# Where the ordinary weight steps stand inside a group of matrix products, how many of them run ahead, and how many tiles of the next group may be loaded

## The chip, the cores and the metric

The kernel runs on one core of one Trainium2 chip. TensorE multiplies, VectorE (DVE) and ScalarE (ACT) work element by element, GpSimd (POOL) and SyncE (SP) mostly issue transfers. The metric is the device time of one execution in microseconds; lower is better. The kernel before took 2078.74 us, the median of three runs between 2076.82 and 2080.69.

## The reference

One layer, 256 rows (tokens) of 2048 numbers, all in float32. A first SwiGLU feed-forward, then attention and retention in parallel with their gates, then a second feed-forward, and a final norm:

```python
def swiglu_ffn(x, w_gate, w_up, w_down):
    return (jax.nn.silu(x @ w_gate) * (x @ w_up)) @ w_down

x = x + 0.5 * swiglu_ffn(rmsnorm(x, norm_ffn1_g), w1_gate, w1_up, w1_down)
h = rmsnorm(x, norm_mix_g)
proj = h @ w_in            # q, k, v of both mixers, and three gates
...
x = x + merged @ w_out
x = x + 0.5 * swiglu_ffn(rmsnorm(x, norm_ffn2_g), w2_gate, w2_up, w2_down)
return rmsnorm(x, norm_final_g)
```

The feed-forwards have 5632 hidden columns. All the weights are read once, some 490 MB.

## The kernel before, in words

**A step.** Every product of activations and weights is cut into steps that hold one weight tile of 256 rows by 512 columns, in SBUF as 128 partitions x 1024 numbers (512 KB). A step's weights are split in two parts: `hi` by a cast on ACT (L128) and `lo`, the rest, by a subtraction on DVE (L129). TensorE then makes three products, `hi` with both parts of the activations (L139, L140) and `lo` with the first (L142). A *standard step* (function `standard`) does this for both halves of 128 rows, twelve matmuls; its tile arrives by a transfer on SP's queue into one of five raw buffers (`RAW_BUFS`).

**A group.** For 10 of the 11 column blocks of each feed-forward, and for the gates of the mixing part, the kernel uses Strassen's scheme on a pair of products (class `Strassen`): seven half-size products in place of eight, at the price of sums of weight tiles. A group has four phases. Phases 0, 1 and 2 have eight *group steps* each, of two kinds that alternate (r: of an operand as it is, s: of a sum), phase 3 has four of kind s. A group step has six matmuls. Its first operands are eight tiles in SBUF, four `k` and four `x`, loaded on POOL's queue (L542). Two of the `x` tiles get the other operand added by an accumulating transfer (L546), the other two by DVE (`first`, L531). In phase 1 each pair also costs DVE an addition (L593) and a subtraction (L579), and POOL an accumulating transfer (`third`, L580). At the end of phase 0 ACT copies PSUM bank `c` away (L636) before phase 1 goes on adding to that bank. After phases 1, 2 and 3 the results are scaled, put through SiLU and multiplied (L639, L642, L650, L653, L765, L768), and a few steps into the next group they are transposed and split as activations (`Operand.put`, L378, L379, L384). These are the operands of the down product.

**The weave.** `weave` writes the order out. It puts `lead` standard steps first, then the groups, and after each pair of group steps it adds to a credit and, if that is high enough, lays in one standard step. So a group has 16 places: four pairs in each of phases 0 to 2 and four single steps in phase 3. The weights of the places are the tuple `SHARE`; the place at the end of phase 2 (`turn`) always gets a step if there is one. In a feed-forward the standard steps are those of the one plain block (gate, then up: 8 steps each), then the down products: 11 passes, one for each column block, of 4 jobs with 2 steps each. A pass may only start some steps after its block's results are there (`at_hand`). A job's second step ends it: ACT then moves two banks out and puts two new ones in, four operations (L785, L788). Fourteen standard steps stay behind the last group. The mixing part has its own lead and shares.

**Running ahead.** `run` goes through the steps in order. Before the matmuls of step c it emits the splits of up to four steps ahead (four `hi`/`lo` buffers, `SPLIT_BUFS`), and with them what else the step's `prep` holds. All engines work their instructions off in this order. `load_some` issues transfers as far as there is room: five raw tiles, and for the groups' first operands as many tiles as `room["kept"]` says. A tile's room comes back when its last split has been emitted, in phases 2 and 3. The tiles themselves come from a pool of 30 (`ACT_TILES`), shared with the 16 parts of the normed activations and with the operands of the down products. The first group's loads may not start before step `first`.

Of the kernel before, what the change touches and what calls it, by code (L numbers as in the profile page):

```python
# [18 lines left out]
D = 2048  # L19
# [7 lines left out]
NB = 512  # L27
KC = 2
# [3 lines left out]
RAW_BUFS = 5  # L32
SPLIT_BUFS = 4
KEPT = 8
ACT_TILES = 30
TAIL = 4
AHEAD = (2, 3)
HALF_K = D // P // 2
LEAD = 12
MIX_LEAD = 8  # L40
RET_WAIT = (14, 5)
HELD = 6

MIX_SHARE = (0.85,) * 4 + (1.0,) * 4 + (0.8,) + (0.4,) * 3 + (0.15,) * 4
SHARE = (0.7,) * 2 + (0.2,) * 2 + (1.3,) * 4 + (0.3,) * 4 + (0.2,) * 4
ADDED = (2, 3)
PLAIN = 10
PASSES = ((10,),) + tuple((b,) for b in range(10))
# [26 lines left out]
def block_kernel(ctx: ExitStack, tc: tile.TileContext, x, g1, w1g, w1u, w1d, gm, w_in, rel, woa, wor, wo,  # L75
# [5 lines left out]
    wpool = ctx.enter_context(tc.tile_pool(name="weights", bufs=1))  # L81
    apool = ctx.enter_context(tc.tile_pool(name="acts", bufs=ACT_TILES))
    tmp = ctx.enter_context(tc.tile_pool(name="tmp", bufs=4))
# [13 lines left out]
    def tmp_tile(name, tag="t", bufs=None):  # L97
        return tmp.tile([P, NB], F32, tag=tag, name=name, bufs=bufs)


    steps = []
    transfers = []
    kept = []
    state = {"dma": 0, "kept": 0, "prep": 0, "step": 0, "slots": SPLIT_BUFS}
    room = {"raw": RAW_BUFS, "kept": KEPT}
    due = {}

    def later(n, fn):
        due.setdefault(state["step"] + n, []).append(fn)
# [114 lines left out]
    def load_some():  # L224
        while state["dma"] < len(transfers) and room["raw"]:
            room["raw"] -= 1
            transfers[state["dma"]]()
            state["dma"] += 1
        while state["kept"] < len(kept) and room["kept"] and kept[state["kept"]][0] <= state["step"]:
            room["kept"] -= 1  # L230
            kept[state["kept"]][1]()
            state["kept"] += 1
# [427 lines left out]
    def down_done(b, factor, after):  # L660
        def done(acc):
            for t in range(NT):
                xb = xs[t][:, b * NB : (b + 1) * NB]
                nc.vector.scalar_tensor_tensor(xb, acc[t], factor, xb, op0=ALU.mult, op1=ALU.add)
            if after is not None:
                after(b)

        return done
# [8 lines left out]

        return done

    def weave(jobs, apart, groups, lead, share, start=None):  # L680


        queue = [(job, k) for job in jobs for k in range(0, job.nk, KC)]
        at_hand = {}

        def next_standard():

            if len(queue) <= apart:
                return False
            job, k = queue[0]  # L690
            if any(at_hand.get(b, len(steps) + 1) > len(steps) for b in job.needs):
                return False
            steps.append(standard(job, k))
            del queue[0]
            if job.makes is not None and k + KC == job.nk:
                at_hand[job.makes] = len(steps) + 6
            return True

        for _ in range(lead):
            next_standard()  # L700
        rate = (len(queue) - apart) / (len(groups) * sum(share))
        credit = 0.0
        first = len(steps) - 8
        for n, (b, make) in enumerate(groups.items()):
            group = make()
            loads = group.loads()
            if start is not None and n == 0:
                loads[0] = lambda load=loads[0]: [start(), load()]
            kept.extend((first + i if n == 0 else 0, fn) for i, fn in enumerate(loads))
            for i, part in enumerate(group.steps()):  # L710
                steps.extend(part)
                credit += rate * share[i]
                if i + 1 == len(share):
                    at_hand[b] = len(steps) + 7

                turn = i + 1 == 3 * (HALF_K // KC)
                if (turn or credit >= (0.2 if (i + 1) % (HALF_K // KC) == 0 else 0.6)) and next_standard():
                    credit -= 1
        for job, k in queue:
            steps.append(standard(job, k))  # L720

    def ffn(name, norm, wg, wu, wd, after, start=None):


        nblocks = DFF // NB
        mids, ready = {}, {}

        def put_mid(b, hs):
            mids[b] = Operand(f"{name}a{b}", 1)
            for t in range(NT):  # L730
                mids[b].put(0, t, hs[t])

        def plain(b):
            gates = {}

            wait = GATE_WAIT if start is not None and b == PLAIN else 0

            def gate_done(acc):
                def go():
                    for t in range(NT):  # L740
                        gates[t] = tmp_tile(f"{name}g{b}{t}", "gate", 2)
                        nc.scalar.activation(gates[t], acc[t], AF.Silu, scale=norm.scale(t))

                if wait:
                    later(wait, go)
                else:
                    go()

            def up_done(acc):
                for t in range(NT):  # L750
                    a = gates[t]
                    nc.vector.scalar_tensor_tensor(a, acc[t], norm.scale(t), a, op0=ALU.mult, op1=ALU.mult)  # L752
                later(4, lambda: put_mid(b, gates))

            tags = ("acc", "acc")
            up = Gemm(wu, 0, b * NB, D // P, norm, up_done, tags)
            up.makes = b
            return [Gemm(wg, 0, b * NB, D // P, norm, gate_done, ("z", "z") if wait else tags), up]

        def paired(b):  # L760
            got = {}

            def evict(t, side, r):
                if side == 1:
                    nc.scalar.activation(r, r, AF.Silu)  # L765
                    got[t] = r
                    return
                nc.vector.scalar_tensor_tensor(got[t], r, norm.scale(t), got[t], op0=ALU.mult, op1=ALU.mult)  # L768
                if t == 1:
                    later(4, lambda: put_mid(b, got))  # L770

            return Strassen(norm, wu, b * NB, wg, b * NB, evict, ADDED)

        def down(blocks, last):

            jobs = []

            def act(k, t):
                return mids[blocks[k // 4]](k % 4, t)

            for b in range(D // NB):
                cols = slice(b * NB, (b + 1) * NB)

                def seed(acc, t, cols=cols):
                    nc.scalar.activation(acc, xs[t][:, cols], AF.Copy, scale=2.0)  # L785

                def evict(acc, t, cols=cols):
                    nc.scalar.activation(xs[t][:, cols], acc, AF.Copy, scale=0.5)  # L788

                if last:  # L790
                    job = Gemm(wd, 0, b * NB, 4 * len(blocks), act, down_done(b, 0.5, after))
                else:
                    job = Gemm(wd, 0, b * NB, 4 * len(blocks), act, None, ("acc", "acc"), seed)
                    job.evict = evict
                job.rows = [(m * 4 + i) * P for m in blocks for i in range(4)]
                job.needs = blocks
                jobs.append(job)
            return jobs

        downs = {blocks: down(blocks, blocks is PASSES[-1]) for blocks in PASSES}  # L800
        jobs = plain(PLAIN) + [job for p in PASSES for job in downs[p]]
        for job, follow in zip(jobs, jobs[1:]):
            job.next = follow
        groups = {b: (lambda b=b: paired(b)) for b in range(nblocks) if b != PLAIN}
        weave(jobs, len(downs[PASSES[-1]]) * len(PASSES[-1]) * 4 // KC + HELD, groups, LEAD, SHARE, start)


    n1 = Norm("n1", gains[:, 0, :], True)
# [3 lines left out]
    def third_block():  # L812

        there = small.tile([P, NB // P], F32, tag="there", name="there", bufs=1)
        nc.gpsimd.tensor_tensor(there, n1.raw[2][:, 0, : NB // P], mhalf, op=ALU.mult)

    ffn("f1", n1, w1g[0], w1u[0], w1d[0], x_updated(nm), third_block)


# [210 lines left out]
    def gates(col1, col2, func, dsts):  # L1030


        def evict(t, side, r):
            if side == 1:
                nc.scalar.activation(r, r, func)
            else:
                bank, r = r, tmp_tile(f"sg{col1}{t}", "gate", 2)
                nc.scalar.activation(r, bank, func, scale=nm.scale(t))
            nc.scalar.dma_start(dsts[side][:, t, :], r)

        return Strassen(nm, w_in0, col1, w_in0, col2, evict)

    both = ("acc", "acc")
    groups = {
        b: (lambda b=b: gates(GA + b * NB, GG + b * NB, AF.Sigmoid, merge_dram[b])) for b in range(D // NB)
    }
# [219 lines left out]
```

## Time and profile before

| | us |
|---|---|
| median of three runs | 2078.74 |
| the profiled execution's own time | 2079.74 |
| its span, from the first to the last instruction | 2078.0 |
| groups of the first feed-forward, start of the first to end of the last | 44.7 to about 665 |
| groups of the second feed-forward | 1412.4 to about 2030 |

Times in the profile count from the span's start. In a row of the timeline the first number is the start, the second the duration, the last, in brackets, the time for which the engine stood idle before it and what ended that. A group bears the number of the step at which it starts: z84 is the group that starts at step 84, and `hiz8410r` is the `hi` part of its phase 1, tile 0, kind r. `x` with a number counts instructions.

### The profile page before, as it was taken

How to read it: one execution, taken by the hardware profiler on the slowest of the kernel's cores; microseconds unless marked ns; L12 is line 12 of the kernel's file. 1: busy time of each engine (PE TensorE's matmuls, PEld its weight loads, DVE VectorE, ACT ScalarE, POOL GpSimd, SP SyncE). 2: the span in 40 equal slices, each digit the busy share in tenths (PEclk: the TensorE clock that was granted, in tenths of full speed). 3: DMA queues.
4: the chain of work that ended last, by engine and by line, in shares of the span. 5: the costliest groups of instructions: out<-in, count | busy, mean ns of one | idle time of the engine just before them, and what ended most of it. 6: DMA issues, size and time to landing. Idle time of an engine off the chain costs nothing. (4 is left out here: it accounts for less than half of the span.)

```text
span 2078.0 us, 26280 instructions
## 1 busy us (share of the span) xinstructions
PE 2047.3 (99%) x9208; PEld 1680.7 (81%) x9208; DVE 1768.2 (85%) x1836; ACT 1490.7 (72%) x1892; POOL 342.3 (16%) x386
## 2 busy tenths in 40 slices
PE   9999999999999999999999999999999999999998
PEld 7777888877888888888888888887878888778877
DVE  7898999989998799899966667568889999889996
ACT  8677888777887767776665434556788787778775
POOL 2221222221122110122100000011122222122210
PEclk9999999999999999999999999999999999999999
DMA  9778889887888777798775645577789888889974
GB/s 325 228 211 247 259 264 289 256 236 226 251 261 251 243 206 258 260 289 252 224 271 174 223 144 189 185 253 181 244 255 291 267 237 231 251 251 272 298 208 132
DMA packets 230325, 498.47 MB, mean 240 GB/s; under 512 B 15584, under 2 KB 16336, under 8 KB 230192
## 3 DMA queue, kind: packets, MB, share of 16 engines
q1 hardware_dynamic: 156736, 301.50, 42.9%
q0 software_dynamic: 70112, 189.44, 35.7%
q10 hardware_dynamic: 3344, 5.84, 0.8%
q8 instruction: 72, 1.18, 0.2%
q14 instruction: 61, 0.50, 0.1%
HBM read 487.81 MB, written 8.91 MB: 239 GB/s over the span
## 5 line engine op out<-in xcount | busy, mean ns | idle before, releaser
L129 DVE TENSOR_TENSOR lo<-raw,hi 128x1024 fp32r<-128x1024 f32 x367 | 447.8, 1224 | 163.4 <-ACT hi L128 161.1
L128 ACT CAST hi<-raw 128x1024 fp32r<-128x1024 f32 x367 | 384.0, 1050 | 206.4 <-PE acc L140 140.0
L788 ACT ACTIVATE xall<-acc 128x512 f32<-128x512 f32 x160 | 94.5, 591 | 17.6 <-PE acc L142 13.1
L785 ACT ACTIVATE acc<-xall 128x512 f32<-128x512 f32 x160 | 95.8, 599 | 15.2 <-DVE f1g L752 7.0
L139 PE MATMUL acc<-hi,mgh 128*128 128x512 f32 x128 | 50.2, 392 | 0.0
L140 PE MATMUL acc<-hi,mgl 128*128 128x512 f32 x128 | 49.8, 389 | 0.0
L139 PE MATMUL acc<-hi,nma01h 128*128 128x512 f32 x96 | 38.6, 403 | 0.0
L139 PE MATMUL acc<-hi,nma00h 128*128 128x512 f32 x96 | 38.6, 402 | 0.0
L140 PE MATMUL acc<-hi,nma00l 128*128 128x512 f32 x96 | 37.5, 390 | 0.0
L139 PE MATMUL acc<-hi,nma10h 128*128 128x512 f32 x96 | 37.5, 390 | 0.0
L140 PE MATMUL acc<-hi,nma01l 128*128 128x512 f32 x96 | 37.5, 390 | 0.0
L140 PE MATMUL acc<-hi,nma11l 128*128 128x512 f32 x96 | 37.4, 390 | 0.0
L139 PE MATMUL acc<-hi,nma11h 128*128 128x512 f32 x96 | 37.4, 390 | 0.0
L140 PE MATMUL acc<-hi,nma10l 128*128 128x512 f32 x96 | 37.4, 390 | 0.0
L142 PE MATMUL acc<-lo,mgh 128*128 128x512 f32 x128 | 35.5, 389 | 0.0
L142 PE MATMUL acc<-lo,nma01h 128*128 128x512 f32 x96 | 29.6, 390 | 0.0
L142 PE MATMUL acc<-lo,nma00h 128*128 128x512 f32 x96 | 29.6, 389 | 0.0
L142 PE MATMUL acc<-lo,nma11h 128*128 128x512 f32 x96 | 29.6, 389 | 0.0
L142 PE MATMUL acc<-lo,nma10h 128*128 128x512 f32 x96 | 29.6, 389 | 0.0
L142 PEld LDWEIGHTS acc<-lo,mgh 128*128 128x128 f32 x128 | 24.0, 188 | 5.0
L140 PEld LDWEIGHTS acc<-hi,mgl 128*128 128x128 f32 x128 | 24.0, 188 | 4.9
L139 PEld LDWEIGHTS acc<-hi,mgh 128*128 128x128 f32 x128 | 24.0, 188 | 4.8
(6634 smaller groups left out, 7144.1 us busy)
## 6 DMA issues: line engine op xcount, KB each, us to landing
raw<-in_ffn_w_down_dram SPq DMA_DIRECT2D x176, 512.0 KB, 6.6
raw<-in_w_in_dram SPq DMA_DIRECT2D x96, 512.0 KB, 4.7
raw<-in_w_out_dram SPq DMA_DIRECT2D x32, 512.0 KB, 4.4
raw<-in_ffn_w_up_dram SPq DMA_DIRECT2D x16, 512.0 KB, 10.3
raw<-in_w_out_att_dram SPq DMA_DIRECT2D x16, 512.0 KB, 4.2
raw<-in_w_out_ret_dram SPq DMA_DIRECT2D x16, 512.0 KB, 4.1
raw<-in_ffn_w_gate_dram SPq DMA_DIRECT2D x15, 512.0 KB, 5.1
z392x<-in_w_in_dram POOLq DMA_DIRECT2D x8, 512.0 KB, 7.5
```

Source lines behind the costliest of these rows:

```text
L128: nc.scalar.copy(hi, raw)
L129: nc.vector.tensor_sub(lo, raw, hi.bitcast(F32))
L139: nc.tensor.matmul(acc, ahi, whi, start=first, stop=False, **more)
L140: nc.tensor.matmul(acc, alo, whi, start=False, stop=False, **more)
L142: nc.tensor.matmul(acc, ahi, wlo, start=False, stop=last, **more)
L785: nc.scalar.activation(acc, xs[t][:, cols], AF.Copy, scale=2.0)
L788: nc.scalar.activation(xs[t][:, cols], acc, AF.Copy, scale=0.5)
```

## The change

Four edits, all in the order of work; no instruction is added or taken away.

1. `SHARE` changes from (0.7, 0.7, 0.2, 0.2 | 1.3 x 4 | 0.3 x 4 | 0.2 x 4) to (0.75 x 4 | 1.0 x 4 | 0 x 4 | 0.2 x 4).
2. The lead of a feed-forward changes from 12 standard steps to 10 in the first and 8 in the second.
3. `weave` raises `room["kept"]` by two at the end of a feed-forward's first group and lowers it again at the end of its last.
4. `first` is now at least 4, which it was before in the first feed-forward; in the second it moves with the lead from step 688 to 684.

```diff
+EXTRA = 2
-LEAD = 12
+LEAD = (10, 8)
-SHARE = (0.7,) * 2 + (0.2,) * 2 + (1.3,) * 4 + (0.3,) * 4 + (0.2,) * 4
+SHARE = (0.75,) * 4 + (1.0,) * 4 + (0.0,) * 4 + (0.2,) * 4
...
-        while state["kept"] < len(kept) and room["kept"] and kept[state["kept"]][0] <= state["step"]:
+        while state["kept"] < len(kept) and room["kept"] > 0 and kept[state["kept"]][0] <= state["step"]:
...
-    def weave(jobs, apart, groups, lead, share, start=None):
+    def weave(jobs, apart, groups, lead, share, start=None, extra=0):
...
+        ends = []
         rate = (len(queue) - apart) / (len(groups) * sum(share))
         credit = 0.0
-        first = len(steps) - 8
+        first = max(len(steps) - 8, D // NB)
...
+            ends.append(len(steps))
+        if extra:
+            due.setdefault(ends[0], []).append(lambda: room.update(kept=room["kept"] + extra))
+            due.setdefault(ends[-1], []).append(lambda: room.update(kept=room["kept"] - extra))
...
-        weave(jobs, len(downs[PASSES[-1]]) * len(PASSES[-1]) * 4 // KC + HELD, groups, LEAD, SHARE, start)
+        weave(jobs, len(downs[PASSES[-1]]) * len(PASSES[-1]) * 4 // KC + HELD, groups, LEAD[start is None], SHARE, start, EXTRA)
```

The rule of the credit can be followed by hand. S is a place that gets a standard step, x one where the credit asks for a step and none is at hand; the four blocks are the phases.

```
group    before, both FFNs      after, first FFN       after, second FFN
0        S..S SSxx SSSS ....    S.SS SSSx xS.S ....    S.SS SSSS ...S ...x
1        .S.S .SSS S.SS ....    S.SS SSSS ...S ....    SS.S SSSS ...S ...S
2        .S.. SSSS S..S ...S    S.SS SSSS ...S ....    .SSS SSSS ...S ....
3        .S.. SSSS S..S ...S    S.SS SSSS ...S ....    .SSS SSSS ...S ....
4        ...S SSSS .S.S ....    S.SS SSSS ...S ....    .SSS SSSS ...S ....
5        S..S SSSS ..SS ....    S.SS SSSS ...S ....    S.SS SSSS ...S ...S
6        .S.S .SSS S.SS ....    S.SS SSSS ...S ....    .S.S SSSS ...S ...S
7        .S.. SSSS S..S ...S    S.SS SSSS ...S ....    .SSS SSSS ...S ....
8        .S.. SSSS S..S ...S    S.SS SSSS ...S ....    .SSS SSSS ...S ....
9        ...S SSSS .S.S ....    S.SS SSSS ...S ....    .SSS SSSS ...S ....
```

The groups of the first feed-forward are z12, z48, z84, z120, z156, z191, z227, z263, z299 and z335 before, those of the second z696, z732, z768, z804, z840, z875, z911, z947, z983 and z1019. The last group of a feed-forward ends at the same step as before, and the total is the same.

## The prediction

> **What bounds the kernel now.** I read the page first, then TensorE's timeline for the pace of one step, then the loss in the two stretches that hold the groups, then TensorE's waits.
>
> ```profile
> PE 2047.3 (99%) x9208; PEld 1680.7 (81%) x9208; DVE 1768.2 (85%) x1836; ACT 1490.7 (72%) x1892; POOL 342.3 (16%) x386
> 61.01 0.39 PE L139 MATMUL z12c<-hiz1210r,n1s3h 128*128 128x512 f32 x1
> 62.37 0.39 PE L139 MATMUL z12c<-hiz1211r,n1s3h 128*128 128x512 f32 x1
> 63.73 0.39 PE L139 MATMUL acc<-hi,n1a01h 128*128 128x512 f32 x1
> 66.45 0.39 PE L139 MATMUL z12a<-hiz1210s,n1s6h 128*128 128x512 f32 x1
> 299.06:357.07 58.01, 58.01 (x262) 48.12 (x260) 54.54 (x51) 47.92 (x60) 11.84 (x13) 1.00 0.86 255
> 44.69:667.40 622.71, 612.27 (x2706) 498.54 (x2705) 568.00 (x529) 487.37 (x595) 128.18 (x138) 1.00 0.85 247
> 1412.43:2030.40 617.97, 609.86 (x2698) 497.29 (x2697) 562.42 (x517) 483.33 (x589) 124.54 (x134) 1.00 0.85 247
> ```
>
> A group step takes 1.36 us (61.01 to 62.37), a standard step 2.72 (63.73 to 66.45), so a matmul 0.2267. Group z156 has 28 group steps and 7 standard ones: 38.08 + 19.04 = 57.12 of its 58.01 us, and the 0.89 left is its eight transposes, 0.11 each. It loses nothing: this pace is the floor. The first FFN's stretch has 2706 records, of which some 81 are transposes: 2625 x 0.2267 + 81 x 0.11 = 604.0 of 622.71, so 18.7 us are lost. The second: 2618 x 0.2267 + 80 x 0.11 = 602.3 of 617.97, 15.7 lost. These 34.4 us are all that a new order can win in the groups. DVE, at 568 of 622.71 (91%), is the close second, so where it falls behind decides.
>
> ```profile
> PE z947c L139 <- ACT z947s L636: 0.8, 1, 0.8
> ...
> PE z299c L139 <- ACT z299s L636: 0.8, 1, 0.8
> PE acc L139 <- ACT hi L128: 2.0, 3, 1.3
> PE acc L142 <- DVE lo L129: 1.7, 5, 0.6
> PE f1a10p L384 <- DVE f1g L752: 1.1, 1, 1.1
> PE z1019c L139 <- ACT hiz101903s L128: 0.5, 1, 0.5
> 189.63 0.39 PE L142 MATMUL z84c<-loz8403s,n1s5h 128*128 128x512 f32 x1
> 190.79 0.50 PE L139 MATMUL z84c<-hiz8410r,n1s3h 128*128 128x512 f32 x1 [0.78 <-ACT z84s L636]
> 191.13 0.40 PE L140 MATMUL z84c<-hiz8410r,n1s3l 128*128 128x512 f32 x1
> ```
>
> The first two lines are the ends of eight like ones (groups 2, 3, 7 and 8 of both FFNs). A wait costs more than its idle time: from 189.63 to 190.79 are 1.16 us in place of 0.23, and the next start is 0.34 later, so 0.78 idle cost 1.04, idle + 0.27.
>
> **The change part by part.**
>
> *A standard step at the end of phase 0.* Phase 1 adds on to the bank that ACT must first copy away (L636). Where a standard step stands in between, its 2.72 us hide the copy: z156 has one and loses nothing. Afterwards every group has an S in that place. Eight waits x 1.04 = 8.3 us go. Without the cover each group would pay 1.04.
>
> *Phases 0 and 1.* These are where DVE falls behind. The precedent is z191, `S..S SSSS`, by phases:
>
> ```profile
> 357.07:374.28 17.21, 17.21 (x81) 14.34 (x80) 16.55 (x17) 14.43 (x19) 1.21 (x1) 1.00 0.65 156
> 374.28:396.04 21.76, 21.76 (x97) 18.02 (x96) 21.76 (x20) 17.24 (x22) 6.80 (x8) 1.00 0.96 243
> 396.04:412.36 16.32, 16.32 (x73) 13.51 (x72) 12.18 (x12) 12.98 (x17) 3.81 (x6) 1.00 1.03 339
> ```
>
> In phase 1 DVE is busy for all of the 21.76 us and TensorE never stops, since DVE enters it ahead. `S.SS` gives DVE a further 2.72 us of cover for one further split, 1.14 (from 171.30 to 177.58 in the rows below DVE does five operations of this size and one of half the size: 6.28 / 5.5). So `SSSS` loses nothing in 18 groups, and `.SSS` in phase 1, to which most of the five waits for `lo` (1.7) belong, is gone.
>
> *Phase 2 with one S in place of two or three.* TensorE has 8 x 1.36 = 10.9 us before the S, DVE 8 splits x 1.14 = 9.1; in z191 ten splits, 11.4, made 12.18 of busy time, so 0.8 of other work comes on top: 9.9. That fits. The S that came late is taken out:
>
> ```profile
> 454.78 2.64 SPq L119 DMA_DIRECT2D raw<-in_ffn_w_down_dram  x3
> 466.84 1.04 ACT L128 CAST hi<-raw 128x1024 fp32r<-128x1024 f32 x1 [4.36 <-DMA raw<-in_ffn_w_down_dram]
> 453.76 1.23 POOL L542 DMA_DIRECT2D z263k<-in_ffn_w_up_dram  x1
> ...
> 462.71 0.72 POOL L542 DMA_DIRECT2D z263x<-in_ffn_w_gate_dram  x1 [2.80 <-DVE loz22721s L129]
> ```
>
> That raw tile took 12.0 us beside POOL's eight loads. It is asked for when the split five raw tiles earlier is done, which for the new turn's S is the last one of phase 1, some 2.6 us before phase 2. Landed by 9.4 and cast by 10.5, it is in time for 10.9, narrowly; at the 8.3 us of z191 with room to spare. Three waits with 2.0 idle, some 2.8 us, go.
>
> *The first wait of a group.* Here something stays.
>
> ```profile
> 168.06 0.60 ACT L785 ACTIVATE acc<-xall 128x512 f32<-128x512 f32 x1
> 169.75 0.58 ACT L788 ACTIVATE xall<-acc 128x512 f32<-128x512 f32 x1
> 170.23 1.04 ACT L128 CAST hiz4833s<-z48x 128x1024 fp32r<-128x1024 f32 x1
> 171.16 1.05 ACT L128 CAST hiz8400r<-z84k 128x1024 fp32r<-128x1024 f32 x1
> 171.30 1.23 DVE L129 TENSOR_TENSOR loz4833s<-z48x,hiz4833s 128x1024 fp32r<-128x1024 f32 x1 [1.72 <-ACT hiz4833s L128]
> 177.58 1.22 DVE L129 TENSOR_TENSOR loz8400s<-z84x,hiz8400s 128x1024 fp32r<-128x1024 f32 x1
> 178.85 0.73 PE L142 MATMUL z84c<-loz8400s,n1s5h 128*128 128x512 f32 x2 [0.53 <-DVE loz8400s L129]
> 352.46 1.23 DVE L129 TENSOR_TENSOR loz15633s<-z156x,hiz15633s 128x1024 fp32r<-128x1024 f32 x1 [0.47 <-ACT hiz15633s L128]
> ```
>
> When the turn's S ends a job, ACT's four bank operations (168.06 to 170.23) stand ahead of the last cast of phase 3, DVE idles 1.72 us and comes late to the new group's third step; when it does not (z156 into z191), DVE idles 0.47 and nothing waits. In the new order every turn of the first FFN ends a job (its groups use exactly eight steps), and the third step is now an S with the same split in the same place of DVE's order. So groups 1 to 9 pay z84's 0.53 + 0.27 = 0.8 each, 7.2; bounds 0 and 1.2 each. In the second FFN only groups 8 and 9 start after such a turn without an S just before: 1.6.
>
> *Shorter leads.* In the first FFN the group starts two steps earlier, and DVE's two additions of `first` with it.
>
> ```profile
> 34.64 1.23 DVE L129 TENSOR_TENSOR lo<-raw,hi 128x1024 fp32r<-128x1024 f32 x1 [1.36 <-ACT hi L128]
> 37.36 1.23 DVE L129 TENSOR_TENSOR loz1200r<-z12k,hiz1200r 128x1024 fp32r<-128x1024 f32 x1 [0.89 <-ACT hiz1200r L128]
> 42.81 1.23 POOL L546 DMA_DIRECT2D z12x<-in_ffn_w_up_dram  x1 [3.41 <-DMA z12x<-in_ffn_w_gate_dram]
> 53.36 1.05 ACT L128 CAST hiz1203s<-z12x 128x1024 fp32r<-128x1024 f32 x1
> 44.69:110.89 66.20, 63.02 (x273) 49.84 (x272) 58.35 (x62) 47.49 (x59) 13.81 (x15) 1.00 0.83 238
> ```
>
> They fit the 2.25 us in which DVE stood idle there (1.36 + 0.89). Without this cover TensorE would wait up to that long. The last accumulate (42.81) had landed by 53.36; the tile's cast comes little earlier now, since one standard step is gone before it and TensorE reaches it 2.72 us sooner. In phase 1 the group now has three S, so DVE reaches the end of the up job, where TensorE waited 1.1 for L752, with more in hand: of the 5.5 us that z12 lost (66.2 less 28 x 1.36, 8 x 2.72 and 0.89) I leave 2.0, bounds 0.5 and 5.5. In the second FFN the up job ends at the turn, before phase 3 with its four splits: its group 0 loses nothing, and I put 1.0 on the start of group 1 (bounds 0 and 2.5). Its loads cannot come sooner:
>
> ```profile
> 1380.69 0.70 POOL L375 TENSOR_TENSOR n2rstd<-v,mhalf 128x2 f32<-128x2 f32 x1 [141.75 <-DVE v L374]
> 1381.34 0.76 POOL L542 DMA_DIRECT2D z696k<-in_ffn_w_up_dram  x1
> 1401.39 1.21 POOL L546 DMA_DIRECT2D z696x<-in_ffn_w_up_dram  x1 [2.64 <-DMA z696x<-in_ffn_w_gate_dram]
> ```
>
> They queue behind the norm's operation already, so `first` = 684 moves nothing. The group starts 10.9 us sooner, at 1401.6; the last accumulate, landed within 10.6 us as in the first FFN (42.81 to 53.36), is there at 1412, and the step that needs it comes at 1416.5. Cost nothing.
>
> *Ten tiles.* Two of the next but one group's loads leave one phase earlier, and with 16 + 10 + 4 tiles the pool of 30 is full, so later loads wait for splits in place of bursting. POOL waits then, and behind it only accumulates that phase 0 needs in its last two steps. I count 0.8 gained, z1019's wait (0.5 + 0.27).
>
> **The sum.** Left are 2.0 + 7.2 + 1.0 + 1.6 = 11.8, and about 1.5 for delays too small for a wait's line: 13.3 of 34.4. With z1019's 0.8 and the others gone, 21.1 go: 2079.74 - 21.1 = 2058.6. That execution stands 1.0 above the median of the runs, so I say 2057.5 (own range 2053 to 2063).
>
> **The rivals.**
>
> *A: the first waits go too.* 2057.5 - 8.8 = 2048.7. For it: two tiles come earlier. Against: z84's first cast (171.16) follows the one before without waiting for a load; it is the bank operations that set DVE back. [...] Chance 0.12.
>
> *B: phase 2 runs dry.* Eight group steps in a row leave DVE no cover; if each of the 19 groups with `...S` lost 0.5, the time were 2067, at 0.9 no change. For it: `lo` ran short in tight stretches (five waits, 1.7). Against: z191's DVE idles a quarter of phase 2. Chance 0.14.
>
> *C: slower, the turn's raw tile is late.* Past 12.4 us from request to landing (2.6 - 1.1 + 10.9) TensorE waits at every turn. It decides from 13.3 us: 0.9 + 0.27 = 1.15, x 19 = 22, the whole gain. At 14 us each costs 1.87, x 19 = 35.5: 2093. For it: 12.0 was seen, and DMA was busy 1.03 in z191's phase 2. Against: POOL's burst is cut by two tiles. Chance 0.05.
>
> *D: the tiles do nothing*, as POOL is held by its accumulates: 2058.3, inside the forecast.
>
> **Chances.** Forecast with D 0.69, A 0.12, B 0.14, C 0.05. A change under 0.2% (4.2 us) cannot be told from none. Faster: forecast, A and B but its tail, 0.91; same 0.05; slower 0.04. The range goes from near A's 2048.7, 2049, to B's 2067; it leaves out part of A, B's tail and C.
>
> **What would show it.** Right: no wait on L636 in any FFN group, none on a raw tile at a turn; nine waits of about 0.5 for `lo` at the third step of the first FFN's groups, two in the second; about 10 us lost against the pace in the first FFN's groups and 4 in the second's. Wrong: waits in phase 2, ACT idle on a raw or a `k` tile, DVE no longer at 100% in phase 1, or POOL's accumulates landing after the cast that needs them.

## The result, and the profile after

The changed kernel takes 2061.73 us, the median of four runs (2061.04 to 2062.25), against 2079.31 for the kernel before beside it: a ratio of 0.9917, 95% interval 0.9904 to 0.9929, faster by 0.8%. The profiled execution took 2061.97 us with a span of 2060.1. The forecast was 2057.5, with an own range of 2053 to 2063. The time is in the range; the runs below show that one term of its sum, the ten tiles, was put far too low, and that the total came out because the change holds them.

The first line of the changed kernel's page, and then phases 0 to 2 of its group z154 by windows (start:end, then the length, then busy us of TensorE, of its weight loads, of DVE, ACT and POOL; then the granted clock, the DMA share and GB/s):

```profile
PE 2037.8 (99%) x9208; PEld 1685.6 (82%) x9208; DVE 1766.2 (86%) x1836; ACT 1494.1 (73%) x1892; POOL 344.8 (17%) x386
```

```profile
290.00:310.80 20.80, 20.27 (x93) 16.52 (x92) 18.62 (x18) 16.67 (x22) 2.73 (x3) 1.00 0.70 193
310.80:332.60 21.80, 21.80 (x98) 18.04 (x97) 21.80 (x21) 17.13 (x22) 6.50 (x7) 1.00 0.94 239
332.60:346.20 13.60, 13.60 (x62) 11.27 (x61) 12.59 (x13) 11.03 (x13) 2.76 (x4) 1.00 1.02 327
```

A group of the first feed-forward now has the same three lengths each time. Phases 1 and 2 run at the pace: DVE is busy in all of phase 1 and in 12.59 of the 13.60 us of phase 2, and TensorE does not stop. What is lost is lost in phase 0.

TensorE's waits in the changed kernel (for what; us in total, times, longest):

```profile
PE acc L143 <- DVE lo L130: 4.9, 9, 0.6
PE z10c L140 <- ACT f1g L748: 2.2, 1, 2.2
PE acc L141 <- DVE f2a10l L380: 1.4, 1, 1.4
...
PE z1018c L143 <- DVE loz101800s L130: 0.6, 1, 0.6
PE z982c L143 <- DVE loz98200s L130: 0.5, 1, 0.5
```

Lines have moved by one (L129 is now the cast, L130 the subtraction, L637 the bank copy). No wait on L637 is left, none on a raw tile at a turn, and the nine and the two first waits are there. Adding what each distance between two matmuls has over the pace (distances less than 0.02 us over it left out), from a group's start to the end of its phase 3, the loss before was 18.5 us in the first feed-forward's groups and 15.9 in the second's (the prediction's 34.4); it is now 13.2 and 4.2. The span fell by 17.9 us.

A turn, z154 into z190, in the timelines of ACT, DVE and TensorE: the four bank operations end, the last cast of phase 3 follows, DVE has stood for 1.88 us, and the third step of the new group waits for its `lo`.

```profile
346.88 0.58 ACT L794 ACTIVATE xall<-acc 128x512 f32<-128x512 f32 x1
347.35 1.04 ACT L129 CAST hiz15433s<-z154x 128x1024 fp32r<-128x1024 f32 x1
348.43 1.22 DVE L130 TENSOR_TENSOR loz15433s<-z154x,hiz15433s 128x1024 fp32r<-128x1024 f32 x1 [1.88 <-ACT hiz15433s L129]
355.98 0.73 PE L143 MATMUL acc<-lo,f1a3h 128*128 128x512 f32 x2 [0.53 <-DVE lo L130]
```

Of the 13.2, 5.0 lie in the first group, z10. First the timelines of POOL, ACT and TensorE there, then the stretches by windows (the granted clock is the third number from the end):

```profile
43.07 1.22 POOL L547 DMA_DIRECT2D z10x<-in_ffn_w_up_dram  x1 [3.00 <-DMA z10x<-in_ffn_w_gate_dram]
44.38 0.72 POOL L376 TENSOR_TENSOR n1rstd<-v,mhalf 128x2 f32<-128x2 f32 x1
45.27 1.28 ACT L748 ACT_TABLE_LOAD   x1
46.57 1.27 ACT L748 ACTIVATE f1g<-acc,n1rstd 128x512 f32<-128x512 f32 x2
47.31 0.50 PE L140 MATMUL z10c<-hiz1000s,n1s5h 128*128 128x512 f32 x1 [2.19 <-ACT f1g L748]
```

```profile
46.00:48.00 2.00, 0.69 (x3) 0.55 (x4) 2.00 (x3) 1.99 (x4) 0.00 (x0) 0.94 1.08 190
48.00:50.00 2.00, 2.00 (x6) 1.60 (x5) 1.44 (x3) 2.00 (x3) 0.00 (x0) 0.50 0.34 61
50.00:52.00 2.00, 2.00 (x8) 1.55 (x7) 2.00 (x4) 1.36 (x3) 0.00 (x0) 0.70 0.04 9
52.00:54.00 2.00, 2.00 (x10) 1.67 (x9) 1.79 (x3) 1.59 (x2) 0.00 (x0) 1.00 0.52 106
```

Bank `c` of the group is one of three PSUM buffers of a tag, and the plain gate product holds two of them until ACT has read them for the SiLU (L748, `gate_done`). With a lead of 10 the group asks for its bank before the norm behind that SiLU is ready. TensorE stands for 2.19 us, and then for 3.4 more, from 47.8 to 51.2, it runs at a granted clock of 0.50 (the 0.70 is the mean of a window in which the clock came back).

### The profile page after: what moved, and what is told of

It is laid out like the page before. It is cut to its first block, busy times and chain, and to the rows that moved or that the text cites. A ratio compares the mean times of both kernels' runs of the same rounds, so it can differ in the third digit from the quotient of the medians.

```text
span 2060.1 us, 26318 instructions
## 1 busy us (share of the span) xinstructions
PE 2037.8 (99%) x9208; PEld 1685.6 (82%) x9208; DVE 1766.2 (86%) x1836; ACT 1494.1 (73%) x1892; POOL 344.8 (17%) x386
## 4 chain that ended last, share of the span: by engine, by line
PE 92%; ACT 3%; DVE 3%; issue 1%; DMA 1%; DVEq 0%; ACTq 0%; POOLq 0%; POOL 0%
PE acc L143 15%; PE acc L140 15%; PE acc L141 15%; DVE lo L130 1%; DMA raw<-in_w_in_dram 1%; ACT hi L129 0%; PE z392a L143 0%; PE z873a L140 0%; PE z910a L141 0%; PE z765a L141 0%; PE z543a L143 0%; PE z430a L143 0%; PE z801a L143 0%; PE z392a L141 0%; PE z505a L143 0%
## 5 line engine op out<-in xcount | busy, mean ns | idle before, releaser
L130 DVE TENSOR_TENSOR lo<-raw,hi 128x1024 fp32r<-128x1024 f32 x367 | 447.1, 1221 | 142.6 <-ACT hi L129 140.8
L129 ACT CAST hi<-raw 128x1024 fp32r<-128x1024 f32 x367 | 384.3, 1051 | 173.3 <-PE acc L141 138.0
```

Source lines behind the costliest of these rows:

```text
L129: nc.scalar.copy(hi, raw)
L130: nc.vector.tensor_sub(lo, raw, hi.bitcast(F32))
```

## The experiments

All are made from the changed kernel by the edits shown. Runs of the kernel before beside them had medians of 2077.8 to 2078.3.

**The three edits, one by one and in pairs.** The edits are the shares (S), the leads (L) and the ten tiles (T). With 16 parts of the normed operand and 4 of the down product's, ten tiles fill the pool of 30.

```diff
 share_only (S)    EXTRA = 0; LEAD = (12, 12)
 leads_only (L)    EXTRA = 0; SHARE as before
 tiles_only (T)    LEAD = (12, 12); SHARE as before
 no_tiles (S, L)   EXTRA = 0
 one_tile          EXTRA = 1
 no_leads (S, T)   LEAD = (12, 12)
 no_share (L, T)   SHARE as before
```

> Only the new shares; the leads stay at 12 and the tiles at eight. Theory 1 (the place of the standard step at the end of phase 0 is what pays, because it covers ACT's copy of the bank): by hand the groups now read S.SS SxxS in the first, then .SSS or S.SS or SS.S in phase 0 with an S at its end in every group, so no wait on the copy at L637 is left in any feed-forward group, and most of the gain is there: about 2064, 2061 to 2068. Bank waits of the first group on the silu at L748 should be absent, since the group starts at step 12, behind the norm. Theory 2 (the shorter leads or the ten tiles are needed to bring the new order about): half of the gain or less, 2070 or more, with waits for lo (L130) and raw tiles in their place.

> Only the shorter leads (10 and 8); old shares, eight tiles. By hand every group of the first feed-forward then reads S..S SSSS .S.S, those of the second still have .S.. without an S at the end of phase 0 in about four groups. Theory 1: the four waits on the copy (L637) of the first feed-forward go, those of the second stay, and the first group pays for its early start as in the changed kernel (a wait of 2 on L748 and a slower clock behind it): about 2071, 2067 to 2075. Theory 2 (the leads alone carry the gain): 2065 or less. Theory 3 (the leads do harm by the first group and bring nothing): 2079 or more.

> Only the ten tiles; old shares and leads. Theory 1: POOL is held by its accumulates and DVE by its order, so two more places change next to nothing: 2077.5 to 2079.5, with the eight waits on L637 (0.8 each) and the waits for lo as before. Rival A (the first waits of a group come from late loads): the five waits for lo go, 2071 or less.

> The changed kernel without the ten tiles (eight as before). Theory 1: the tiles are worth 0 to 1, so 2061.5 to 2063, and the nine waits of about 0.5 for lo at L143 in the first feed-forward stay as they are. Rival (the new order needs the earlier loads, since the pool of thirty is what feeds phase 0): waits on first operands' tiles appear, 2066 or more.

> The changed kernel with nine tiles in place of ten. With eight, the cast of phase 0's last tile waits about 3 for its accumulating transfer in six or more groups, and the time is 2080; with ten that wait is gone. Theory 1 (it is a matter of how many bytes must still come between the groups, with no cover of standard steps in phase 2): one tile of 512 KB takes some 2.1 at the 247 GB/s of these groups, so nine tiles leave a lateness of about 1, and most of DVE's head start is kept: between the two, 2064 to 2072. Theory 2 (a threshold: the tile that decides is loaded on time or not): 2062 as with ten, or 2079 as with eight.

> New shares and ten tiles, leads of 12 as before. Theory 1 (shares and tiles carry the gain together, the leads only give the pattern): with the shares alone the profile showed late accumulates (about 3 in six groups) and a loss of 7.7 and 5.2 in phase 1 of the two first groups, where the operand of the up block is needed; the tiles remove the former, not the latter: 2064 to 2070. Theory 2 (the shares are bad without the shorter leads, tiles or not): 2075 or more.

> Shorter leads and ten tiles, old shares. The shorter leads alone gave 2067.5 with four waits of 0.8 on the bank copy in the second feed-forward and two late loads. Theory 1 (the tiles matter only where phase 2 has one standard step, and here it has two): the tiles bring 0.5 to 2, so 2065.5 to 2067, and the shares' own part of the gain is about 4 to 5. Theory 2 (the tiles are worth as much here as under the new shares): 2055 or less.

| kernel | us (median) | ratio to before, 95% | loss in groups, first / second feed-forward |
|---|---|---|---|
| before | 2078.3 | | 18.5 / 15.9 |
| T | 2075.67 | 0.9981 to 0.9999 | 16.0 / 13.8 |
| L | 2067.46 | 0.9936 to 0.9961 | 13.5 / 9.9 |
| S | 2082.63 | 1.0009 to 1.0027 | 17.0 / 18.5 |
| L, T | 2067.81 | 0.9938 to 0.9963 | 13.5 / 10.7 |
| S, T | 2068.31 | 0.9940 to 0.9965 | 13.2 / 12.6 |
| S, L (eight tiles) | 2080.06 | 1.0002 to 1.0020 | 22.3 / 10.6 |
| S, L, nine tiles | 2065.73 | 0.9928 to 0.9955 | 14.7 / 7.7 |
| S, L, T (the change) | 2061.73 | 0.9904 to 0.9929 | 13.2 / 4.2 |

The losses are those of the one profiled execution each; with eight tiles that one took 2077.68, 2.4 less than the median. Two of my theories fell. The shares alone are slower than before, though they do remove every wait on L637 in the feed-forwards as foreseen. And the tiles, which I held to be worth at most 1, are worth 18.3 us under the new shares and leads (2080.06 to 2061.73), 14.3 under the new shares alone (2082.63 to 2068.31), 2.6 by themselves and nothing under the leads alone (2067.46 to 2067.81). The leads by themselves bring 10.8, which I had foreseen at about 7: in the first feed-forward the groups then have an S at the end of phase 0 without new shares (`S..S SSSS .S.S`); in the second four waits on L637 stay.

What the tiles do is seen in ACT's waits, and in one turn with eight and with ten.

ACT's waits with eight tiles (the two ends and one between of eight like rows):

```profile
ACT hiz83703s L129 <- DMA z837x<-in_ffn_w_up_dram: 3.8, 1, 3.8
ACT hiz19003s L129 <- DMA z190x<-in_ffn_w_up_dram: 3.2, 1, 3.2
...
ACT hiz87302s L129 <- DMA z873x<-in_ffn_w_up_dram: 2.4, 1, 2.4
```

Eight tiles, the timelines of POOL, ACT and DVE at z190, whose phase 0 starts at 354.0:

```profile
355.99 1.23 POOL L547 DMA_DIRECT2D z190x<-in_ffn_w_up_dram  x1 [12.21 <-DMA z190x<-in_ffn_w_gate_dram]
360.06 1.21 POOL L547 DMA_DIRECT2D z190x<-in_ffn_w_up_dram  x1 [2.84 <-DMA z190x<-in_ffn_w_gate_dram]
367.94 1.05 ACT L129 CAST hiz19003s<-z190x 128x1024 fp32r<-128x1024 f32 x1 [3.22 <-DMA z190x<-in_ffn_w_up_dram]
369.02 1.23 DVE L130 TENSOR_TENSOR loz19003s<-z190x,hiz19003s 128x1024 fp32r<-128x1024 f32 x1 [2.07 <-ACT hiz19003s L129]
```

The same kernel, how long the loads of z190's `x` tiles took from issue to landing, from the answer on that tile, and then phases 0 and 1 by windows:

```profile
DMA to landing us min/median/max: 6.0/14.2/18.7
```

```profile
354.00:375.20 21.20, 20.45 (x94) 16.36 (x92) 17.02 (x17) 15.47 (x21) 2.44 (x2) 1.00 0.73 191
375.20:398.50 23.30, 22.99 (x97) 17.84 (x98) 23.30 (x21) 17.91 (x23) 6.29 (x7) 1.00 0.86 224
```

Ten tiles, the changed kernel, z190 again, whose phase 0 starts at 351.6: the timelines, the `x` tiles' loads, and phase 1 by windows:

```profile
349.29 1.23 POOL L547 DMA_DIRECT2D z190x<-in_ffn_w_up_dram  x1 [11.60 <-issue]
352.97 1.22 POOL L547 DMA_DIRECT2D z190x<-in_ffn_w_up_dram  x1 [2.45 <-DMA z190x<-in_ffn_w_gate_dram]
362.65 1.06 ACT L129 CAST hiz19003s<-z190x 128x1024 fp32r<-128x1024 f32 x1 [0.30 <-PE z190c L141]
```

```profile
DMA to landing us min/median/max: 6.5/10.5/15.6
```

```profile
372.40:394.20 21.80, 21.80 (x98) 18.04 (x97) 21.80 (x21) 17.14 (x22) 6.49 (x7) 1.00 0.94 240
```

Counted from the group's start, the two accumulates are issued at 2.0 and 6.1 us with eight tiles and at -2.3 and 1.4 with ten. With eight the last one lands too late for its cast, by 3.2 us; DVE stands for 2.07 us at the end of phase 0, enters phase 1 without what it had in hand, and is then busy for all of the 23.30 us while TensorE waits for it. The new shares leave phase 2 one standard step, 13.6 us, where it had two, 16.3, or more. The eight loads wait for room that comes back about when phase 2 starts. Counted from the start of the phase 2 ahead of z190, the cast of that last tile comes at 30.1 in the changed kernel, in which it waits for no load, but with eight tiles the accumulate lands at 32.9. In the kernel with the leads alone (L), whose phase 2 has two standard steps and which has eight tiles too, the accumulates are issued at -2.1 and 2.1 from the group's start, the last one lands at 29.9 by the first count, and the cast comes at 31.4. So under the new shares the cast comes 1.4 us sooner and the accumulate lands 3.0 later; why it lands that much later is not shown. In the kernel before, ACT waited for a fourth tile's accumulate too, but for 0.8 (z335) and 0.7 (z1019) at most. Nine tiles give 2065.73, with five such waits of 1.3 to 2.6 in the first feed-forward and one of 5.0 in the last group: the price falls by degrees, 18.3, 4.0 and nothing, and no threshold is seen.

The leads of 12 cost the first group instead. In the kernel with S and T, TensorE's waits:

```profile
PE acc L141 <- DVE f1a10l L380: 1.9, 1, 1.9
PE acc L141 <- DVE f2a10l L380: 1.9, 1, 1.9
```

The up block then ends at the first S of phase 1, where DVE has most to do (it is busy for all of the 21.80 us of that phase in z154 of the changed kernel), and the first down product wants its operand there: the first groups of the two feed-forwards lose 7.4 and 6.8 us, against 5.0 and 0.1 in the changed kernel (`f1a10l` and `f2a10l` are the `lo` part of that operand in the first and the second feed-forward). The shorter leads move that end, to the third S of phase 1 in the first feed-forward and to the turn in the second.

**What makes the first waits.** Odd leads set the pattern one step off against the jobs of two steps, so that the turn's step ends no job; eight held steps in the second feed-forward do the reverse.

```diff
 odd_turns      LEAD = (11, 8); held back 5 in the first feed-forward, 6 in the second
 even_turns2    LEAD = (10, 8); held back 6 and 8
 odd_mixed      LEAD = (11, 9); held back 5 and 7
```

> In the changed kernel the lead of the first feed-forward becomes 11 and one step less is held back behind its last group, so that the same pattern S.SS SSSS ...S stands one step off against the jobs of two steps: the step at each turn no longer ends a job, and ACT's four bank operations move away from the end of phase 3. Theory 1 (the nine waits for lo are made by these bank operations standing ahead of the cast): all nine waits at L143 vanish, 9 x 0.8 = 7.2 less; the first group starts one step later, so its bank wait of 2.2 on L748 falls below 0.5 and the slow clock behind it goes, but the up block's end falls behind the turn, about 1 to 2 back. Time about 2053, 2050 to 2056. Rival (a group's eighth standard step or late loads make these waits): they stay, and only the first group changes: 2058 to 2061.

> In the changed kernel the lead of the second feed-forward stays at 8 and eight steps in place of six are held back behind its last group, so that its groups use eight standard steps each and every turn's step ends a job, as in the first feed-forward. Theory 1 (the bank operations at the turn cost 0.8 per group): six or seven more waits of 0.5 to 0.6 for lo at L143 in the second feed-forward, 5 to 6 more: about 2067, 2065 to 2069. Rival: they come from something of the first feed-forward alone, and the time stays at 2061 to 2063.

> Turn steps that end no job in both feed-forwards, without the earlier squares: leads 11 and 9, five and seven steps held back. From the profile of the first variant (2053.8) the second feed-forward should lose its 1.4 before the operand of the up block and its two waits for lo, 1.5 and 1.6 together: 2050.5, 2049.5 to 2052. If the second feed-forward's gain in the variant with both was an effect of the earlier squares, 2053 to 2054.

`odd_turns` took 2053.8 us (ratio 0.9870 to 0.9897), `even_turns2` 2067.52 (0.9938 to 0.9963), `odd_mixed` 2050.78 (0.9855 to 0.9882). TensorE's waits on `lo`, first in `odd_turns`, then in `even_turns2`:

```profile
PE acc L143 <- DVE lo L130: 0.6, 1, 0.6
```

```profile
PE acc L143 <- DVE lo L130: 9.5, 17, 0.6
```

Nine waits went from the first feed-forward, and the loss of its groups 1 to 9 fell from 8.2 to 1.0 (by the groups' lengths from 8.0 to 0.2: the sum of distances keeps some 0.1 a group where nothing waits); the one that is left is in the first group. That group, starting a step later, no longer waits for its bank, but loses 5.3 us, 3.7 of them in phase 1, where the up block ends; in the changed kernel it lost 5.0. There the expected gain did not come. In the other kernel the second feed-forward's loss rose from 4.2 to 9.5. The turn of `odd_turns` in ACT's and DVE's timeline:

```profile
331.74 0.60 ACT L791 ACTIVATE acc<-xall 128x512 f32<-128x512 f32 x1
332.27 0.58 ACT L794 ACTIVATE xall<-acc 128x512 f32<-128x512 f32 x1
344.92 1.06 ACT L129 CAST hiz15533s<-z155x 128x1024 fp32r<-128x1024 f32 x1 [0.63 <-PE acc L141]
346.01 1.23 DVE L130 TENSOR_TENSOR loz15533s<-z155x,hiz15533s 128x1024 fp32r<-128x1024 f32 x1
```

The bank operations lie 12 us ahead of the last cast, and DVE has no idle time before its subtraction, where z154 of the changed kernel has 1.88. So the bank operations at the turn are the cause, shown in both directions, and the loads are not. The second feed-forward has the closest pair: in `even_turns2` and `odd_mixed` its groups 2 to 9 have the same pattern of S, and the turn's step ends a job in the one and not in the other; by their lengths they lose 7.5 us and nothing. `odd_mixed` moves the bank operations off the turn in both feed-forwards and is the fastest kernel here. There a whole group takes 60.70 us and loses next to nothing, as z155 shows by windows (phase 0, and the sum over its four phases):

```profile
290.60:310.50 19.90, 19.90 (x93) 16.59 (x92) 18.59 (x19) 16.46 (x21) 2.74 (x3) 1.00 0.79 212
...
sum 60.70, PE 60.70 PEld 50.38 DVE 56.57 ACT 49.50 POOL 13.20; mean PE 15.18 PEld 12.59 DVE 14.14 ACT 12.37 POOL 3.30
```

**The bank of the first group.** `early_silu` moves the squares of the norm and the SiLU forward; `odd_both` adds odd leads in both feed-forwards.

```diff
 early_silu   GATE_WAIT = 2
-        at(D // NB * 2 + b, lambda b=b: [n1.square(b, t) for t in range(NT)])
+        at(D // NB * 2 - 3 + b, lambda b=b: [n1.square(b, t) for t in range(NT)])
 odd_both     the same, and LEAD = (9, 9); held back 7 and 7
```

> In the changed kernel the squares of the first norm stand three steps earlier (steps 5 to 8 in place of 8 to 11) and the gate's end waits two steps in place of five, so that ACT reads the gate's bank (L748) before phase 0 of the first group needs it. Theory 1: the wait of 2.2 on L748 goes, and the stretch at a granted clock of 0.5 behind it goes with it, 3.5 to 4 together: about 2058, 2056.5 to 2059.5, with a clock of 1.00 from 44 to 54. If the clock falls there all the same, the idle stretch is not its cause, and only 2.2 go (2059.5). Rival (the group simply starts too early for its loads): the stall moves to an accumulate or a cast of the first tiles, 2061 or more.

> The parity of the odd turns in both feed-forwards (leads 9 and 9, seven steps held back in each), together with the earlier squares and silu. Theory 1: no turn's step ends a job, so the nine waits for lo in the first feed-forward and the two in the second go (11 x 0.8 = 8.8), and the bank wait with its slow clock (3.8) goes too; the first group starts one step earlier than in the changed kernel, which may leave its last accumulated tile late by up to 2.5. Time 2049 to 2053. Rival (the waits belong to the groups' loads): 2058 or more, with the waits for lo still there.

`early_silu` took 2065.23 us (2063.19 to 2065.59), slower than the changed kernel, and `odd_both` 2053.13, hardly faster than `odd_turns` and 2.4 slower than `odd_mixed`, which has odd leads in both feed-forwards without the earlier squares. The wait on L748 is gone and the clock is 1.00 from 40 to 58 us, so that half of the theory holds. But the rival holds too, by a way that I had not seen. POOL in `early_silu`:

```profile
39.37 0.72 POOL L376 TENSOR_TENSOR n1rstd<-v,mhalf 128x2 f32<-128x2 f32 x1 [14.65 <-DVE v L375]
40.05 0.75 POOL L543 DMA_DIRECT2D z10x<-in_ffn_w_gate_dram  x1
...
48.53 1.23 POOL L547 DMA_DIRECT2D z10x<-in_ffn_w_up_dram  x1 [2.05 <-DVE n1f L495]
```

The norm's operation now stands ahead of three of the group's loads in POOL's order. POOL waits 14.65 us for DVE's sum, the loads go out behind it, and the last accumulate is issued at 48.53 where it was 43.07. The group lost 5.0 us before and 5.7 now. The profiled execution is the fastest of its five; why the others are up to 2.4 us longer is not settled.

The bank wait and the slow clock do not account for the first group's loss by themselves. In `even_turns2` the bank wait is the same, but the clock stays full behind it (last section). Here are phases 0 and 2 of z10 by windows, first there, then in the changed kernel:

```profile
39.16:60.69 21.53, 19.34 (x86) 15.69 (x85) 18.83 (x25) 19.53 (x30) 2.48 (x3) 1.00 0.62 156
79.72:99.08 19.36, 18.50 (x81) 14.04 (x80) 17.77 (x19) 15.74 (x20) 7.04 (x9) 1.00 1.04 313
```

```profile
39.51:62.64 23.13, 20.93 (x85) 16.82 (x84) 20.41 (x26) 19.77 (x30) 2.50 (x3) 0.93 0.62 162
81.68:99.76 18.08, 17.56 (x82) 14.19 (x80) 16.48 (x18) 15.75 (x20) 5.96 (x9) 1.00 1.03 324
```

Phase 0 is 1.60 us shorter there, but phase 2 is 1.28 longer, and the group loses 4.6 in place of 5.0. In phase 1 between them, 19.04 long in both kernels, DVE is busy all the time. So what is spared in phase 0 is mostly lost again later. That DVE sets the pace of this group is likely, but no run here takes it apart.

## Why the prediction was right, and where it was wrong

- **L636 (8.3 to go), the raw tile (2.8), phases 0 and 1 without loss, phase 2 with one S.** All seen with ten tiles: no wait on the copy in a feed-forward group, none on a raw tile at a turn, and of groups 1 to 9 of both feed-forwards none loses anything in phases 1 and 2. With eight tiles it is not so: "`SSSS` loses nothing" fails by 9.6 us in phase 1 of those groups (11.0 by the lengths of these phases).
- **Ten tiles: "I count 0.8 gained".** This is the step that failed. I took the accumulates behind POOL's waits for harmless since phase 0 needs them only in its last two steps. They are the very transfers that come late once phase 2 is 13.6 us long (3.2 us at z190 with eight tiles). The precedent, z191, came behind a phase 2 with two S, that of z156, 16.3 us long, and so showed phases 0 and 1 with the loads on time. The effect was 18.3. The total came out all the same because I had booked that gain under the shares, where the cover by S was taken to be enough. That the change held the two tiles is luck as far as this forecast goes: by its reasoning they could have been left out, and the time would have been 2080.06, far outside the range.
- **Rival D, that the tiles do nothing (2058.3),** is refuted by the run without them (2080.06). Rival A named the tiles, but for another wait: the first waits stayed with ten tiles and went with the odd leads. For the accumulates the room for two more tiles did count: the last one 3.2 us late for its cast with eight, in time for it with ten.
- **First waits, 7.2 and 1.6.** Nine and two came, at 0.53 to 0.6 idle; with small delays the nine groups lost 8.2, the two 1.8. Cause as predicted, shown by `odd_turns` and `even_turns2`.
- **Shorter leads, first feed-forward, 2.0 left (bounds 0.5 to 5.5).** Measured 5.0. I watched DVE's two additions, which cause no wait of TensorE, and did not ask who holds the PSUM bank that the group wants. In phase 0 some 2.4 are that wait and 1.6 the slower clock. But `even_turns2` without the slow clock lost 4.6, and `odd_turns` and `early_silu` without the bank wait 5.3 and 5.7, so what keeps this group at about 5 stays open.
- **Second feed-forward, 1.0 on the start of group 1 (bounds 0 to 2.5).** Measured 1.75, most of it the wait of 1.39 for f2a10l: DVE takes it up at 1460.54, behind the group's additions. In `odd_mixed` it is 0.2. That its first group loses nothing was right (0.09).
- **Rivals B and C** did not happen: phase 2 does not run dry, and no turn waits for a raw tile.

So 17.4 us were left in the groups where I had 13.3, which is about the 4.2 between 2057.5 and 2061.73.

## What to carry to other kernels

When a change has several parts, forecast each part also without the others: here the order that removes the waits is slower than before until the next loads have room, and the room is worth little without the order (2.6 us by itself, nothing beside the leads alone). A precedent stretch vouches only for what it contains; look at what came just before it, above all at the time in which the next transfers had to land. And before work is started earlier, ask of each resource that it takes, PSUM banks included, who still holds it (2.19 us for the bank here), and of each queue what is moved ahead of what (POOL stood for 14.65 us at the norm's operation, with the loads behind it).

## What the runs showed of the hardware

TensorE's granted clock fell to 0.50 behind a pause of about 2 us in some of the kernels, and stayed full behind a like one in others. The same wait of 2.19 us on L748 is followed by 0.50 in the changed kernel (rows above) and by full clock in `even_turns2`:

```profile
48.00:50.00 2.00, 2.00 (x10) 1.67 (x9) 1.56 (x2) 1.88 (x3) 0.00 (x0) 1.00 0.11 19
```

In that kernel phase 0 of z10 lost 2.46 us in place of 4.07, so by my estimate the slow stretch costs some 1.6 in that phase, of which 0.4 is left over the whole group (4.6 in place of 5.0). Behind the same pause the kernel with leads alone fell to 0.50 as well (from 48 to 50 us), the one with eight tiles (2.23 us) stayed at 1.00. In the kernels S and S, T the clock fell behind the 1.9 us for f1a10l, with waits of 0.9 and 0.5 for L758 just ahead of it: from 84 to 86 us its mean is 0.50 in S and 0.58 in S, T. So the length of the pause does not decide it alone: 1.9 us, with the shorter waits ahead, was followed by 0.50 in two kernels, and 2.23 was not in a third. What else decides is not settled here.
